# A transformer block with expert retrieval: six more expert blocks made ahead, four block buffers, and another order and pacing of VectorE's work

## The chip, the cores and the metric

The kernel runs on one core of a Trainium2 chip. The metric is the device time of one execution in microseconds (us), lower is better. The time before is the median of three runs.

## The reference, cut to what matters

One encoder block on 1024 tokens of width 1024: attention and a convolution first, then a retrieval layer over 16384 experts (128 blocks of 128). The second half is what the change touches:

```
def _peer(xn, peer_wq, peer_keys, peer_u, peer_v):
    ...
        q = (xc @ peer_wq).reshape(TOKEN_CHUNK, PEER_HEADS, PEER_DQ)
        s1 = jnp.einsum('chd,nd->chn', q[..., :half], peer_keys[0])
        s2 = jnp.einsum('chd,nd->chn', q[..., half:], peer_keys[1])
        v1, i1 = lax.top_k(s1, PEER_TOPK)
        v2, i2 = lax.top_k(s2, PEER_TOPK)
        ...
        top_s, pos = lax.top_k(cand_s, PEER_TOPK)
        e = jnp.take_along_axis(cand_i, pos, axis=-1)
        g = jax.nn.softmax(top_s, axis=-1).astype(xc.dtype)
        u = peer_u[e]
        h = jax.nn.gelu(jnp.einsum('cd,chkd->chk', xc, u))
        return jnp.einsum('chk,chkd->cd', g * h, peer_v[e])
```

Each token picks 16 experts for each of 8 heads, 128 in all.

## The kernel before, in words

The 1024 tokens are 8 tiles of 128. Two methods share the retrieval layer.

**Gathered tiles.** Tiles 0, 1 and 2 (`NG = 3`) take the direct way: for each of the 128 picks of a token, GpSimd issues an indirect DMA (L1154) that fetches one row of 1024 values for each of 128 tokens, and VectorE multiplies and sums it (L1187, for `peer_u`) or adds it with its weight (L1199, for `peer_v`). That is 3 x 256 = 768 gathers. `class Gather` keeps their order, 7 row slots and the pointer `nc`.

**Dense tiles.** Tiles 3 to 7 (640 tokens, `TD`) take the dense way: all 128 blocks of 128 experts are multiplied with all tokens. For a block, 48 matmuls (8 slices of the width, 3 passes of a split in two halves, 2 token halves) give the block's activations, ScalarE applies Gelu, VectorE multiplies them with the gate matrix, and matmuls with the block's `peer_v` rows add the result into the outputs. The gate matrix is built from the picks by matmuls of one-hot matrices, 160 groups of four tokens, and stored in DRAM (`GD`).

The program's order is written out by hand, and the instructions of an engine run in the order in which they are issued. Four stages follow each other.

1. Attention, convolution and projections, up to the scores of the retrieval (`wgen`), which are stored in DRAM (`SD`).
2. The **second stage**, the loop that calls `gpe`, `ustep`, `gpost` and `kadv`. An iteration issues one one-hot group on TensorE (`gpe`: three matmuls for the differences, L1082 to L1085, and eight for the product, L1100), a quarter of an activation block that is made ahead (`ustep`: 12 matmuls, L1236), ScalarE's work for the one-hot groups (`gprep`, L1091 and L1093, and `gevac`, L1110, which copies the product into one of five buffers `gblk`; every eighth iteration stores four of them, L1113), and then some of VectorE's work (`kadv`). The loop ends when all 160 groups are done. Blocks made ahead are stored in DRAM (`HDm`).
3. A short **junction**: the last two ahead blocks, the first loads and splits of the last stage.
4. The **last stage**, a loop over blocks i = 0 to 126. An iteration has three slots. A slot holds `rotate` (six matmuls of 512 columns over two blocks into the one PSUM tile `prot`, which VectorE then adds into the output X, L1561), `accum` (three matmuls, in the third slot six, into `acc`), and `ugroup` (12 matmuls, L1496, a quarter of an activation block that was not made ahead). Between them stand VectorE's gate products (L1479, L1487) and the gathers, which are spread evenly over the iterations (`gat.adv`).

**What sets the order around the change.** `K0` blocks are made ahead (their indices are `US`, evenly spread), all but `KT = 2` of them in the second stage: `KM = K0 - KT`, so 31 blocks and 124 calls of `ustep`. The other 95 blocks (`ulist`) are made in the last stage, 380 quarters for 381 slots. `kadv` keeps a credit for VectorE: an iteration adds its modelled length (3.05), and each step of VectorE's work that `kstep` issues takes its price off: 2.0 for a head of the first top-k (`topk1`), 1.3 or 1.8 for the pieces of the second (`topk2`, L986 at its start, L1037 near its end), `GCOST = 3.0` for a gather. `kstep` takes the second top-k before the first one and gathers last, but after a piece of the second top-k lets another kind go first. `korder` is the order of the tiles in both top-ks: dense tiles' picks feed the one-hot groups, gathered tiles' picks feed the gathers, and no gather can be issued until the picks of tile 0 are there. Inside `topk2` a dense tile's values go through ScalarE (the exponential at L1012, then 24 copies into `L`, spread over nine iterations by `HOLD`), in ScalarE's order ahead of its one-hot work.

The multiply of a `peer_u` gather writes its full product, which nobody reads, into the third part of the tile `QB` (`jk`); only the sum is kept. The activations of the last stage live in three buffers (`hfree`): two tiles and the first part of `QB`. A buffer is taken by `hload` (a block made ahead is loaded, L1453) or by `ugroup` (Gelu writes it), and given back by `amake2`. `uahead` splits the next block's weights into two halves (`usplit`: a copy on ScalarE, L116, and a subtraction on GpSimd, L119) once an iteration.

Of the kernel before, what the change touches and what calls it, by code (L numbers as in the profile page):

```python
# [10 lines left out]
BF = mybir.dt.bfloat16  # L11
# [3 lines left out]
ALU = mybir.AluOpType  # L15
# [16 lines left out]
NK = 128  # L32
# [9 lines left out]
NPERS = 4  # L42
K0 = 33
WIN = 2
NVI = 3
NO2 = 2
GPE = 1.4
GCOST = 3.0
KT = 2
# [22 lines left out]
def peer_block(tc, I, out):  # L72
# [54 lines left out]
    with ExitStack() as fr:  # L127
# [55 lines left out]
        with ExitStack() as st:  # L183
# [186 lines left out]
            for j, nm in enumerate(["q_norm_g", "k_norm_g"]):  # L370
                a = I[nm]
# [120 lines left out]
        with ExitStack() as st:  # L492
# [272 lines left out]
            for u in range(NU + 4):  # L765
                g = (u + 4) // 4
# [350 lines left out]
    class Gather:  # L1117
# [51 lines left out]
        def adv(self, n=1):  # L1169
            for _ in range(n):  # L1170
# [7 lines left out]
                if ph == 0:  # L1178
                    h = self.h(t) if ps is None else ps
                    if k == 0:  # L1180
                        self.hh[t] = gp.tile([P, P], F32, name=f"hh{t}")
                        if ps is not None:
                            self.stage(t)
                            A.copy(ps, self.staged[t])
                            self.slots.append(self.staged.pop(t))
                    jk = QB[:, 2, :].bitcast(BF)
                    V.scalar_tensor_tensor(jk, r, 1.0, h, op0=ALU.mult, op1=ALU.mult,  # L1187
                                           accum_out=self.hh[t][:, k:k + 1])
# [57 lines left out]

    korder = [3, 4, 5, 0, 6, 7, 1, 2]
    ks = dict(n1=0, n2=0, gen=None, ld=0, credit=0.0, last="")
# [36 lines left out]
    def k_gat():  # L1285
        if not ks.get("gat") or not gat.ready():
            return None
        gat.adv(1)
        return GCOST

# [52 lines left out]
    ust = dict(i=0, seg=0, hps=None, prev=None)  # L1343

    def ustep():
        i = ust["i"]
        if i >= KM:
            return 0.0
        if i == 0 and ust["seg"] == 0:
# [54 lines left out]
    while True:  # L1404
# [6 lines left out]
        kadv(dt, dt)  # L1411
    ho = gelu_(ust["prev"], up, 1)
    SY.dma_start(HDm[KM - 1], ho[:])
    while ks["n2"] < len(korder):
# [4 lines left out]
    with ExitStack() as vs:  # L1419
# [47 lines left out]
        hfree = [vp.tile([P, TD], F32, name=f"ho{j}")[:] for j in range(2)]  # L1467
        hfree.append(QB[:, 0:2, :].rearrange("p a b -> p (a b)")[:, :TD])

# [45 lines left out]
        ulist = [i for i in range(NK) if i not in UI]  # L1515
        ug = dict(g=0, split=0, load=0, ps=None)

# [9 lines left out]
        def ugroup():  # L1527
# [3 lines left out]
            i, (hf, d) = ulist[m], divmod(q, 2)  # L1531
            if ug["split"] <= m:
                uahead()
            if d == 0:
                ug["ps"] = ubank()
            uhalf(i, hf, ug["ps"], d * DC // 2, (d + 1) * DC // 2)
            if d == 1:
                if hf == 0:
                    HO[i] = hfree.pop(0)
                ugelu(HO[i], hf, ug["ps"])  # L1540
            ug["g"] += 1

        def uready(i):
# [56 lines left out]
        for i in range(NK - 1):  # L1600
# [9 lines left out]
            vsplit(nx)  # L1610
            uahead()
            rs_ = [w for w in range(len(rot)) if i % WIN == w % WIN]
            rotate(rs_[0], i, False)
            accum(i, (0,))
            ugroup()
            gat.adv(gs[0])
            rotate(rs_[1], i, False)
            accum(i, (1,))
            ugroup()
            uready(nx)  # L1620
# [4 lines left out]
            accum(i, (2, 3))  # L1625
            ugroup()
            gat.adv(gs[2])
# [73 lines left out]
```

## Time and profile before

| | |
|---|---|
| median of 3 runs | 2993.06 us (2991.23 to 2999.02) |
| the profiled execution | 2996.14 us, span 2994.4 us, mean granted TensorE clock 0.979 |
| busy over the span | TensorE 2799.0 us (93%), VectorE 2463.6 (82%), GpSimd 1953.6 (65%), ScalarE 1149.2 (38%) |
| DMA | 710.33 MB, mean 237 GB/s |
| chain of work that ended last | TensorE 55%, VectorE 20%, DMA 8%, issue 7% |

A busy time is the time in which an engine had at least one instruction in work; matmuls overlap, and their ends are modelled. In a row of the trace, PE is TensorE's matmuls, PEld its weight loads, DVE VectorE, ACT ScalarE, POOL GpSimd, SPq the DMA queue that SyncE issues. "a <- b" names what was waited for; L numbers are lines of the kernel.

### The profile page before, as it was taken

What the parts mean: (1) busy time and instruction counts of PE and PEld (TensorE: products, weight loads), DVE (VectorE), ACT (ScalarE), POOL (GpSimd) and SP (SyncE); (2) the same over time, 40 slices, a digit from 0 to 9 for tenths busy, and PEclk for the clock granted to TensorE, in tenths of its full rate; (3) what the DMA queues carried; (4) which work ended last, traced back from release to release, by engine and by line L of the source; (5) the groups of instructions that cost most, each with busy time, mean ns of one, the idle gap of its engine ahead of it and who ended that gap; (6) DMA issues with size and microseconds to landing.
All of it is one profiled execution on the core that took longest, in us unless ns stands there. A gap on an engine that the chain in (4) does not pass through costs nothing.

```text
span 2994.4 us, 44528 instructions
## 1 busy us (share of the span) xinstructions
PE 2799.0 (93%) x16042; PEld 2475.3 (83%) x16048; DVE 2463.6 (82%) x4465; ACT 1149.2 (38%) x2376; POOL 1953.6 (65%) x1558
## 2 busy tenths in 40 slices
PE   7878899899989899978999999999999999999997
PEld 6767778698978788867888888888888888888886
DVE  5889988468666967864899988988899999999998
ACT  3216566342577577663222222222222222222222
POOL 2578842104445766764777777777777777777775
PEclk9989999999999999999999999999999999999999
DMA  4111000044334667676899898999999998989996
GB/s 131 46 68 36 8 1 15 33 159 129 106 142 149 219 228 266 211 276 251 330 336 345 332 337 330 349 334 353 335 348 335 349 347 333 341 333 337 341 342 228
DMA packets 296719, 710.33 MB, mean 237 GB/s; under 512 B 25264, under 2 KB 135216, under 8 KB 296368
## 3 DMA queue, kind: packets, MB, share of 16 engines
q0 software_dynamic: 110592, 402.70, 35.2%
q1 hardware_dynamic: 156800, 252.85, 25.1%
q10 hardware_dynamic: 29104, 51.91, 4.6%
q8 instruction: 126, 2.06, 0.3%
q14 instruction: 97, 0.79, 0.1%
HBM read 640.46 MB, written 66.91 MB: 236 GB/s over the span
## 4 chain that ended last, share of the span: by engine, by line
PE 55%; DVE 20%; DMA 8%; issue 7%; POOL 4%; ACT 4%; ACTq 1%; SPq 0%; another core or an unknown queue 0%; POOLq 0%; DVEq 0%
PE hps L1496 15%; PE hps L1236 5%; PE prot L122 5%; PE prot L123 4%; PE prot L124 4%; DVE y L146 3%; PE pg L1100 3%; PE acc L122 3%; PE acc L124 3%; PE acc L123 3%; DMA rows<-peer_v,ei 2%; DMA rows<-peer_u,ei 2%; DVE ga L1199 2%; DVE ho L1479 2%; DVE PT L119 2%
## 5 line engine op out<-in xcount | busy, mean ns | idle before, releaser
L1496 PE MATMUL hps<-HN,uh 128*128 128x320 f32 x3072 | 683.9, 310 | 8.1 <-ACT ho L1243 5.3
L1496 PEld LDWEIGHTS hps<-HN,uh 128*128 128x128 f32 x3072 | 530.4, 189 | 42.4 <-issue 5.5
L1496 PE MATMUL hps<-HN,ul 128*128 128x320 f32 x1536 | 475.6, 310 | 0.0
L1199 DVE SCALAR_TENSOR_TENSOR ga<-rows,aa,ga 128x1024 f32<-128x1024 f32 x330 | 424.0, 1285 | 27.5 <-DMA rows<-peer_v,ei 18.1
L1154 POOL DMA_INDIRECT rows<-peer_u,ei x339 | 360.1, 1062 | 108.0 <-issue 68.7
L119 POOL TENSOR_TENSOR vl<-vr,vh 128x1024 fp32r<-128x1024 f32 x128 | 308.8, 2413 | 156.9 <-ACT vh L116 108.5
L1154 POOL DMA_INDIRECT rows<-peer_v,ei x330 | 326.9, 991 | 112.6 <-issue 72.5
L1187 DVE SCALAR_TENSOR_TENSOR QB<-rows,ga 128x1024 bf16<-128x1024 f32 x271 | 329.7, 1216 | 31.3 <-DMA rows<-peer_u,ei 25.1
L122 PE MATMUL prot<-vh,ah 128*128 128x512 f32 x762 | 309.0, 406 | 27.9 <-DVE X L1561 18.6
L119 POOL TENSOR_TENSOR ul<-ur,uh 128x1024 fp32r<-128x1024 f32 x127 | 324.5, 2555 | 2.6
L1561 DVE TENSOR_TENSOR X<-X,prot 128x512 f32<-128x512 f32 x384 | 262.1, 682 | 65.5 <-PE prot L124 55.2
L123 PE MATMUL prot<-vl,ah 128*128 128x512 f32 x762 | 301.1, 395 | 0.4 <-POOL vl L119 0.4
L124 PE MATMUL prot<-vh,al 128*128 128x512 f32 x762 | 297.5, 390 | 0.0
L1496 PEld LDWEIGHTS hps<-HN,ul 128*128 128x128 f32 x1536 | 289.5, 188 | 0.0
L1506 ACT ACTIVATE ho<-hps 128x320 f32<-128x320 f32 x128 | 55.8, 436 | 493.3 <-PE hps L1496 456.2
L1110 ACT COPY gblk<-pg 128x128 f32<-128x128 f32 x640 | 175.6, 440 | 99.2 <-PE pg L1100 74.2
L116 ACT CAST vh<-vr 128x1024 fp32r<-128x1024 f32 x128 | 133.7, 1045 | 203.3 <-DMA vr<-peer_v 196.0
L1236 PE MATMUL hps<-HN,uh 128*128 128x320 f32 x992 | 210.0, 334 | 0.0
L122 PE MATMUL acc<-vh,ah 128*128 128x512 f32 x512 | 199.6, 390 | 0.0
L124 PE MATMUL acc<-vh,al 128*128 128x512 f32 x512 | 199.6, 390 | 0.0
L123 PE MATMUL acc<-vl,ah 128*128 128x512 f32 x512 | 199.5, 390 | 0.0
L122 PEld LDWEIGHTS prot<-vh,ah 128*128 128x128 f32 x762 | 143.2, 188 | 65.7 <-DVE X L1561 32.6
(273 smaller groups left out, 6550.0 us busy)
## 6 DMA issues: line engine op xcount, KB each, us to landing
ur<-peer_uT SPq DMA_DIRECT2D x128, 512.0 KB
vr<-peer_v SPq DMA_DIRECT2D x128, 512.0 KB
GD<-gblk ACTq DMA_DIRECT2D x80, 512.0 KB
gl<-GD SPq DMA_DIRECT2D x64, 640.0 KB
wqr<-peer_wq SPq DMA_DIRECT2D x32, 512.0 KB
HDm<-ho SPq DMA_DIRECT2D x31, 320.0 KB
s<-SD SPq DMA_DIRECT2D x64, 128.0 KB
ho<-HDm SPq DMA_DIRECT2D x22, 320.0 KB
```

Of the source, the lines that this page charges most:

```text
L116: A.copy(hi, src)
L119: lo_eng.tensor_tensor(lo, src, f(hi), op=ALU.subtract)
L122: PE.matmul(ps, ah, bh, start=start, stop=False)
L123: PE.matmul(ps, ah, bl, start=False, stop=False)
L124: PE.matmul(ps, al, bh, start=False, stop=stop)
L1110: A.copy(gblk[b][k][:, :, q * 4:q * 4 + 4].rearrange("p i t -> p t i"), pg[:, :, k * w:k * w + w])
L1154: G.indirect_dma_start(out=r, out_offset=None, in_=I["peer_v" if ph else "peer_u"], in_offset=bass.IndirectOffsetOnAxis(ap=ge[t][:, k:k + ...
L1187: V.scalar_tensor_tensor(jk, r, 1.0, h, op0=ALU.mult, op1=ALU.mult, accum_out=self.hh[t][:, k:k + 1])
L1199: V.scalar_tensor_tensor(to, r, self.aa[t][:, k:k + 1], to, op0=ALU.mult, op1=ALU.add)
L1236: PE.matmul(hps[:, j, :b - a], (uh, uh, ul)[st3][:, dc, :], HN[(0, 1, 0)[st3]][:, dc, a:b], start=dc == 0 and st3 == 0, stop=dc == DC - 1 ...
L1496: PE.matmul(ps[:, :b - a], (uh, uh, ul)[st3][:, dc, :], HN[(0, 1, 0)[st3]][:, dc, a:b], start=dc == 0 and st3 == 0, stop=dc == DC - 1 and ...
L1561: V.tensor_tensor(X[:, NG + t, n:n + 512], X[:, NG + t, n:n + 512], pr, op=ALU.add)
```

## The change

It makes 39 instead of 33 blocks ahead (37 of them, 148 calls of `ustep`, in the second stage), so 89 are left for the last stage (356 quarters for 381 slots). `uslot` issues a quarter only when the count of quarters lags an even spread over all slots, and not when it would need the last free buffer. The product of a `peer_u` gather is written over the gathered row itself; the whole of `QB` then gives two activation buffers, four in all. `uahead` moves from the start of an iteration to behind the first quarter of a block. Tile 0 comes third in `korder` instead of fourth, tile 5 fourth. A gather costs 2.0 of credit. `ulast` stores the last ahead block of the second stage.

```diff
-K0 = 33
+K0 = 39
...
-GCOST = 3.0
+GCOST = 2.0
+GCOST2 = 2.0
...
-                    jk = QB[:, 2, :].bitcast(BF)
-                    V.scalar_tensor_tensor(jk, r, 1.0, h, op0=ALU.mult, op1=ALU.mult,
+                    V.scalar_tensor_tensor(r, r, 1.0, h, op0=ALU.mult, op1=ALU.mult,
                                            accum_out=self.hh[t][:, k:k + 1])
...
-    korder = [3, 4, 5, 0, 6, 7, 1, 2]
+    korder = [3, 4, 0, 5, 6, 7, 1, 2]
...
-        return GCOST
+        return GCOST if ks["n2"] < len(korder) else GCOST2
...
+    def ulast():
+        if ust["prev"] is not None:
+            ho = gelu_(ust["prev"], up, 1)
+            SY.dma_start(HDm[KM - 1], ho[:])
+            ust["prev"] = None
+
     def ustep():
         i = ust["i"]
         if i >= KM:
+            ulast()
             return 0.0
...
-        hfree.append(QB[:, 0:2, :].rearrange("p a b -> p (a b)")[:, :TD])
+        hfree += [QB[:].rearrange("p a b -> p (a b)")[:, j * TD:(j + 1) * TD] for j in range(2)]
...
-            if ug["split"] <= m:
-                uahead()
             if d == 0:
                 ug["ps"] = ubank()
...
             ug["g"] += 1
+            if q == 0:
+                uahead()
+
+        def uslot():
+            ug["slot"] += 1
+            if ug["g"] < -(-4 * len(ulist) * ug["slot"] // (3 * (NK - 1))) and (ug["g"] % 4 != 1 or len(hfree) > 1):
+                ugroup()
...
             vsplit(nx)
-            uahead()
             rs_ = [w for w in range(len(rot)) if i % WIN == w % WIN]
             rotate(rs_[0], i, False)
             accum(i, (0,))
-            ugroup()
+            uslot()
...
             accum(i, (1,))
-            ugroup()
+            uslot()
...
             accum(i, (2, 3))
-            ugroup()
+            uslot()
```

## Rows read from the trace of the kernel before

**Rows 1.** Busy time by stretch: span bounds, length, each engine's busy time, clock, DMA share, GB/s
```profile
853.50:1295.10 441.60, 417.67 (x2844) 376.73 (x2843) 331.13 (x1189) 310.37 (x868) 284.84 (x230) 0.99 0.60 210
1295.10:1363.20 68.10, 46.42 (x259) 33.18 (x257) 38.51 (x50) 48.10 (x145) 32.64 (x22) 0.89 0.68 250
1363.20:1399.70 36.50, 33.16 (x176) 30.79 (x177) 14.75 (x24) 10.63 (x15) 17.99 (x12) 0.88 0.75 259
1399.70:2962.70 1563.00, 1543.49 (x8271) 1364.48 (x8270) 1416.69 (x1756) 383.39 (x541) 1215.15 (x907) 1.00 0.91 338
```

**Rows 2.** Chain that ended last, second stage: start, length, engine, tile, line
```profile
1041.10 0.91 PE pg L1100 x8
...
1151.47 0.91 PE pg L1100 x8
...
1200.31 1.75 PE hps L1236 x12
1203.60 1.76 PE hps L1236 x12
...
1356.74 1.17 PE pg L1100 x8
```

**Rows 3.** Groups by line and shape, 853 to 1363 us: busy, mean ns, idle before
```profile
L1110 ACT COPY gblk<-pg 128x128 f32<-128x128 f32 x592 | 162.5, 441 | 94.9 <-PE pg L1100 74.2 <-DMA GD<-gblk 18.1 <-remote 2.2
L1187 DVE SCALAR_TENSOR_TENSOR QB<-rows,QB 128x1024 bf16<-128x1024 f32 x68 | 100.0, 1471 | 26.7 <-DMA rows<-peer_u,ei 26.0 <-issue 0.2
L1154 POOL DMA_INDIRECT rows<-peer_u,ei x73 | 90.6, 1241 | 20.7 <-issue 12.7 <-DVE QB L1187 1.4 <-DVE z L1032 1.3
L119 POOL TENSOR_TENSOR ul<-ur,uh 128x1024 fp32r<-128x1024 f32 x30 | 84.1, 2805 | 2.4
```

**Rows 4.** Waits in the second stage and, last, of SyncE's queue in the last stage
```profile
ACT d L1012 <- DVE d L1011: 4.9, 1, 4.9
...
POOL uh L118 <- PE hps L1236: 103.4, 19, 17.4
...
SPq L1453 <- DVE ho L1479: 459.2, 21, 24.5
```

**Rows 5.** VectorE in order of time: start and end of tile 6's and tile 7's second top-k
```profile
977.72 0.45 DVE L986 CAST xf<-ix 128x256 f32<-128x256 uint32 x1
...
1039.94 0.29 DVE L1037 TENSOR_TENSOR g<-d,rz 128x128 f32<-128x128 f32 x1
...
1074.47 1.23 DVE L986 CAST xf<-ix 128x256 f32<-128x256 uint32 x1
...
1144.35 1.91 DVE L1037 TENSOR_TENSOR g<-d,rz 128x128 f32<-128x128 f32 x1
```

**Rows 6.** Chain that ended last, an iteration of the last stage
```profile
1611.23 1.75 PE hps L1496 x12
1612.99 0.23 PE prot L122
...
1615.05 1.75 PE hps L1496 x12
...
1619.55 1.75 PE hps L1496 x12
```

**Rows 7.** Groups by line, 1399.7 to 2962.7 us
```profile
L1199 DVE SCALAR_TENSOR_TENSOR ga<-rows,aa,ga 128x1024 f32<-128x1024 f32 x327 | 420.1, 1285 | 27.4 <-DMA rows<-peer_v,ei 18.1 <-issue 2.7 <-DVE X L1561 0.9
L1187 DVE SCALAR_TENSOR_TENSOR QB<-rows,ga 128x1024 bf16<-128x1024 f32 x265 | 322.4, 1216 | 29.8 <-DMA rows<-peer_u,ei 23.6 <-issue 2.1 <-DVE X L1561 0.4
L1561 DVE TENSOR_TENSOR X<-X,prot 128x512 f32<-128x512 f32 x376 | 256.6, 682 | 60.3 <-PE prot L124 50.1 <-issue 8.6
L122 PEld LDWEIGHTS prot<-vh,ah 128*128 128x128 f32 x752 | 141.1, 188 | 53.3 <-DVE X L1561 22.0 <-issue 7.7 <-DVE ga L1199 4.0
```

**Rows 8.** Line L1435, a multiply that writes whole f32 rows: ns min/median/max
```profile
L1435 DVE SCALAR_TENSOR_TENSOR rows<-X,rs,rows x6: 1277/1278/1283, 2972.0 to 2987.2; 128x1024 f32<-128x1024 f32 x6
```

**Rows 9.** TensorE in order of time at the start of the junction
```profile
1364.97 0.73 PE L1496 MATMUL hps<-HN,uh 128*128 128x320 f32 x2
...
1365.77 0.73 PE L1496 MATMUL hps<-HN,uh 128*128 128x320 f32 x2
```

More of the change, by code (lines that the diff above doesn't have):

```diff
@@ L1411, in peer_block @@
         kadv(dt, dt)
-    ho = gelu_(ust["prev"], up, 1)
-    SY.dma_start(HDm[KM - 1], ho[:])
+    ulast()
     while ks["n2"] < len(korder):
@@ L1515, in peer_block @@
         ulist = [i for i in range(NK) if i not in UI]
-        ug = dict(g=0, split=0, load=0, ps=None)
+        ug = dict(g=0, split=0, load=0, ps=None, slot=1)
         def uahead():
```

## The prediction

> **What bounds the kernel now.** I read the busy time by stretch first, because the shares of the whole span mix stages with different limits. In the last stage TensorE is busy for 1543.5 of 1563.0 us, VectorE for 1416.7 (90.6%), and the DMA engines for 91% [rows 1]: TensorE sets the time, with two others close behind. In the second stage TensorE is busy for 417.7 of 441.6 us, until its last ahead block ends at 1295.1. Then follow 68.1 us in which only one-hot groups are left and TensorE is busy for 46.4 us at a granted clock of 0.89 [rows 1]. Those 68 us are the room that the change wants to fill. 124 of the loop's iterations hold a quarter block, and the loop has 148: 13 of the 160 groups are done in stage one, 147 are left, one an iteration, and one iteration drains. 37 blocks are 148 quarters, so the new ones fill exactly the 24 bare iterations, and the loop gets no longer in count.
>
> **Second stage, six blocks added.** The chain of waits shows two neighbouring quarters 3.29 us apart, and the same point four batches of eight iterations later 110.4 us apart, so 3.45 us an iteration with the batch's stores [rows 2]. The last one-hot group starts 61.6 us after 1295.1 [rows 2]. With quarters in them, the same 23 intervals take 23 x 3.45 = 79.4 us: **+18 us**. The ends are 23 x 3.29 = 75.7 (+14) and 23 x 3.56 = 81.9 (+20), the mean of the first 124 (441.6/124). The waits of ScalarE for stores of the gate matrix, 18.1 us [rows 3], lie mostly in the bare iterations and shrink with the slower pace; that is in the 3.45. Six more block stores and loads stand on SyncE's queue here, as before one a block.
>
> **Second stage, gathers and order.** Following the credits step by step through the pacing code gives 68 gathers before the loop ends, which is what the trace has [rows 3], and 108 after: 40 more, all of tile 0's first half. They cost VectorE 40 x 1.47 = 59 us and GpSimd 40 x 1.24 = 50 us, and six more subtractions cost GpSimd 17 us [rows 3]. VectorE is busy for 331.1 + 38.5 = 369.6 of 509.7 us now; it would be 429 of some 528 (81%). GpSimd's queue, which carries casts, subtractions, top-k sums and gathers in one order, waits 103.4 us for TensorE to free a weight buffer [rows 4]; the 67 us fit into that. So on average neither bounds. What counts is where ScalarE stands waiting for VectorE inside the second top-k, with the one-hot work queued behind it and TensorE behind that. Before, this cost 4.9 us once [rows 4]. By the credits, a dense tile's second top-k gets 16 iterations from its start to its hand-over in place of 18, because gathers go by faster and tile 0 no longer comes between the dense tiles: 55 us for what took VectorE 62.2 and 69.9 us [rows 5]. Some of those were waits for GpSimd that TensorE held back. I take **+4 us**, between 0 and 44 (three tiles, 7 and 15 us late each). One head of the first top-k slips from stage one into stage two; it is in that share.
>
> A gather's multiply takes 1471 ns in the second stage, where both operands lie in SBUF, and 1216 ns in the last stage, where one lies in PSUM [rows 3, 7]: 0.255 us more for each of the 40, 10 us of VectorE's time that the move costs, already in the 59. The Trainium skill (SBUF — State Buffer, section "Who interferes with whom") has a rule for it, and it speaks against this move: a VectorE instruction with two SBUF inputs contends with a GpSimd instruction that reads SBUF, and the second to issue waits. By that rule more GpSimd work in the stage makes every such multiply, the old ones too, longer still.
>
> **Last stage, 24 quarters less.** Here a quarter takes 1.76 us from its start to the next matmul, and an iteration without a stall 3.82 + 4.50 + 3.82 = 12.14 us [rows 6]. 24 x 1.76: **-42 us**. VectorE loses 40 gathers at 1.30 (52 us) and the DMA 40 rows' worth and net one block's worth of bytes (22 MB, 65 us at the 338 GB/s of [rows 1]). All three near-limits go down by at least what TensorE does, so none takes over by its sum.
>
> **The gaps that the missing quarters leave.** `prot` is one PSUM tile: the next rotation cannot start until VectorE has added the last one. A quarter and three `accum` matmuls cover that now for 2.28 us (0.52 without the quarter; 1.20 in the third slot). The addition takes 0.68 us [rows 7] and ends 0.73 us after the rotation if VectorE is free: 0.2 us of stall. If a gather of 1.29 us has just begun, 1.5 us. Stepping the even spread through gives 8, 9 and 7 skips in the three slots: 17 x 0.85 + 7 x 0.4 = 17 us. I take **+14**, since VectorE's load falls to (1417 - 52)/(1563 - 31) = 89%; ends 5 and 42, the second being all that was saved. The stalls of this kind that exist, 22.0 us before the rotation's weights [rows 7], shrink with the load: **-3** (0 to -10).
>
> **Junction and clock.** The junction's first matmuls run with the triplets 0.80 us apart where 0.44 (a quarter of the 1.76) is the pace later, at a granted clock of 0.88, after TensorE had idled; some six triplets [rows 9]. With the stage before filled, TensorE comes in busy: **-2 us**.
>
> **Edits that I cost at nothing.** The product written as a whole f32 row: a multiply with such an output takes 1278 ns against 1216 [rows 8, 7]; 276 of the last stage's would cost 17 us at most, and none at least; VectorE's idle 146 us there cover it, and without that cover it would add to the gaps. `uahead` one to three slots later: a split then leads its block by three slots (11.5 us), more than its copy and subtraction of under 4 us; if a load came late, the block's first matmul would wait. The fourth buffer: `hload` waits 459 us in SyncE's queue for a buffer [rows 4], with weight loads behind it, but none of TensorE's long waits is for a weight; it makes the even spread possible, no more. `ulast`: one Gelu in the same place.
>
> **Sum.** 18 + 4 - 42 + 14 - 3 - 2 = -11 us, against the profiled execution's 2996.1 us. That one lies 3.1 us above the median, so on the median's scale 2993 - 11 = 2982 us.
>
> **The rivals.**
> (1) *Slower: ScalarE waits for VectorE at each dense tile's hand-over.* If the three second top-ks need the measured 62 to 70 us in 55, the loop loses 7 to 15 us at each, 33 us in the middle in place of my 4: -11 - 4 + 33 = +18, so 3011 us. It decides from a total lateness of some 24 us on. For it speak the two spacings [rows 5] and the longer multiplies; against it VectorE's 72% load and the 103 us for which GpSimd waits.
> (2) *No change that can be told.* The second stage grows by 20 + 8 and the gaps give back 16, with no relief for the old stalls: 28 - 42 + 16 - 2 = 0, so 2993 us. For it speaks that each term is only somewhat worse than mine.
> (3) *A larger gain.* VectorE's lower load closes most gaps: 14 + 0 - 42 + 5 - 6 - 2 = -31, so 2962 us. For it speaks that VectorE is relieved by more than TensorE; against it that a skipped slot always leaves at least 0.2 us.
> By the skill's rule alone, the second stage's old 68 multiplies would rise by a like 0.25 us, 17 us of VectorE's time, an estimate; that is a push towards rival 1, and its chance includes it.
>
> **How the numbers follow.** My forecast has 0.40 and covers 2972 to 2984. Rival 2 has 0.28 (2984 to 3002), rival 3 0.17 (below 2972), rival 1 0.15 (above 3002). 0.3% is 9 us, about what a measurement of this kernel can tell from no change. So faster has 0.40 + 0.17 = 0.57, the same 0.28, slower 0.15. The range leaves out a tenth at each side: 2964, near rival 3's middle, to 3004, into rival 1.
>
> **What would show it.** 108 gathers with their target row as output before the junction, and 37 ahead blocks; the quarters of the last 24 iterations 3.4 to 3.5 us apart and the junction's start near 1379 to 1386 us; a granted clock near 1.00 at that start. The last stage shorter by 25 to 36 us, with VectorE's share at 89% or less, and waits of the rotation for VectorE's addition up by some 10 us. I am wrong on the second stage if ScalarE waits for VectorE (L1012, L1063) by 20 us or more, and wrong on the last stage if it shrinks by under 20 us or by the full 42.

## The result, and the profile after

The kernel became slower: 3077.32 us in the median of five runs (3062.88 to 3084.38) against 2993.06, a ratio of 1.0275 (1.0248 to 1.0302). I had forecast 2982, and the result lies outside my range. The profiled execution took 3062.88 us, 66.7 more than that of before (2996.14); it is the fastest of the five, 14.4 us under the median.

Busy time by stretch of the changed kernel, with the columns of [rows 1] (PE, PEld, VectorE, ScalarE and GpSimd busy, granted clock, DMA share, GB/s): second stage, junction, last stage, end.

```profile
858.60:1397.00 538.40, 499.06 (x3390) 449.50 (x3388) 459.34 (x1399) 361.60 (x1012) 408.33 (x317) 0.98 0.69 246
1397.00:1433.00 36.00, 27.74 (x145) 25.79 (x146) 9.56 (x17) 8.67 (x13) 15.98 (x11) 0.86 0.85 301
1433.00:3027.20 1594.20, 1520.57 (x8006) 1338.75 (x8005) 1355.61 (x1685) 372.86 (x525) 1164.54 (x866) 0.99 0.88 319
3027.20:3061.10 33.90, 17.26 (x63) 13.06 (x61) 23.55 (x27) 11.05 (x19) 7.85 (x16) 0.75 0.31 125
```

Against [rows 1], the start of the second stage moved by 5.1 us (858.6 for 853.5), the second stage grew by 28.7 (509.7 to 538.4), the junction went from 36.5 to 36.0, and the end grew by 2.2. **The last stage, with 24 quarter blocks less to do, grew by 31.2 us** (1563.0 to 1594.2), where I had forecast about 31 less. In it TensorE stands idle for 73.6 us (1594.2 - 1520.6) in place of 19.5, VectorE's share fell from 90.6% to 85%, and the DMA's from 0.91 to 0.88. No engine took over as the bound: everything waits more.

Where the waits are. Waits in the last stage of the changed kernel, 1450 to 3020 us (us in total, times, longest), and under them those of SyncE's own DMA queue:

```profile
ACT vh L117 <- DMA vr<-peer_v: 242.6, 38, 13.4
POOL vl L120 <- ACT vh L117: 182.8, 41, 11.5
PEld prot L123 <- DVE X L1572: 71.0, 59, 5.2
PE prot L123 <- DVE X L1572: 50.8, 38, 4.8
PE hps L1502 <- ACT ho L1512: 12.8, 6, 6.1
...
SPq L1218 <- POOL ul L120: 902.8, 76, 18.4
SPq L1459 <- DVE ho L1485: 311.4, 34, 20.0
SPq L1463 <- POOL vl L120: 78.9, 19, 10.5
SPq L1463 <- DMA vr<-peer_v: 39.2, 9, 6.9
```

L1459 is the load of the gate matrix `gl` (L1453 before), L1463 the load of a block's `peer_v` rows `vr` (L1457), L117 ScalarE's copy that splits them (L116). ScalarE had waited for `vr` before, too. Its queue in order of time, before, at each fourth block:

```profile
1574.57 1.05 ACT L116 CAST vh<-vr 128x1024 fp32r<-128x1024 f32 x1 [6.60 <-DMA vr<-peer_v]
1624.26 1.06 ACT L116 CAST vh<-vr 128x1024 fp32r<-128x1024 f32 x1 [6.36 <-DMA vr<-peer_v]
1674.49 1.05 ACT L116 CAST vh<-vr 128x1024 fp32r<-128x1024 f32 x1 [7.18 <-DMA vr<-peer_v]
1724.78 1.05 ACT L116 CAST vh<-vr 128x1024 fp32r<-128x1024 f32 x1 [6.84 <-DMA vr<-peer_v]
```

and after:

```profile
1568.75 1.05 ACT L117 CAST vh<-vr 128x1024 fp32r<-128x1024 f32 x1 [6.14 <-DMA vr<-peer_v]
1624.82 1.04 ACT L117 CAST vh<-vr 128x1024 fp32r<-128x1024 f32 x1 [13.41 <-DMA vr<-peer_v]
1674.36 1.05 ACT L117 CAST vh<-vr 128x1024 fp32r<-128x1024 f32 x1 [6.28 <-DMA vr<-peer_v]
1726.64 1.05 ACT L117 CAST vh<-vr 128x1024 fp32r<-128x1024 f32 x1 [5.42 <-DMA vr<-peer_v]
...
2337.41 1.05 ACT L117 CAST vh<-vr 128x1024 fp32r<-128x1024 f32 x1 [10.79 <-DMA vr<-peer_v]
```

Before, one such wait stands every 50 us, that is every fourth iteration, and nearly all of them are 6 to 7 us long. After, they swing between 1 and 13 us. What happens in the longest of them, SyncE's queue first, then ScalarE, VectorE and TensorE, in order of time (start, length; in brackets the idle time before it and what ended it):

```profile
1603.97 0.33 SPq L1218 DMA_DIRECT2D ur<-peer_uT  x1
1604.34 6.29 SPq L1459 DMA_DIRECT2D gl<-GD  x2
1610.68 5.27 SPq L1463 DMA_DIRECT2D vr<-peer_v  x2
...
1610.69 0.73 ACT L1487 CAST ah<-ho 128x640 fp32r<-128x640 f32 x1 [2.43 <-DVE ho L1485]
1624.82 1.04 ACT L117 CAST vh<-vr 128x1024 fp32r<-128x1024 f32 x1 [13.41 <-DMA vr<-peer_v]
1625.77 0.43 ACT L1512 ACTIVATE ho<-hps 128x320 f32<-128x320 f32 x1
...
1609.75 0.90 DVE L1485 TENSOR_TENSOR ho<-ho,gl 128x320 f32<-128x320 f32 x2
...
1626.26 0.90 PE L1502 MATMUL hps<-HN,uh 128*128 128x320 f32 x2 [6.11 <-ACT ho L1512]
```

Read from the top. The gate load comes in two halves and has three buffers, so its second half has to wait until VectorE's gate product of the block before (L1485, 1609.75) gives a buffer back. SyncE's queue is in order: the `vr` load, which needs nothing from the gate, is issued only at 1610.68, and its data are there at 1624.8, 14 us later (over the whole run a `vr` load lands after 8.4 us in the median). ScalarE is in order as well: it stands at the copy of `vr` for 13.41 us, and behind that copy stands the Gelu (L1512) that empties TensorE's one bank `hps`. So TensorE waits 6.11 us for a bank that ScalarE could have emptied long before.

In the kernel before, the `vr` load stands behind the gate load as well, but there the first gate half has gone out long ahead of it:

```profile
1744.11 23.35 SPq L1453 DMA_DIRECT2D gl<-GD  x2
1767.56 0.60 SPq L1457 DMA_DIRECT2D vr<-peer_v  x1
```

In the changed kernel a weight load (L1218) had held the queue until 1604, because GpSimd's subtraction had not yet freed its buffer. SyncE's waits from 1600 to 1620 us:

```profile
SPq L1218 <- POOL ul L120: 13.5, 1, 13.5
```

So both gate halves went out just ahead of `vr`. From 1450 to 2900 us the two halves are issued 21.7 us apart in the median before, and 10.0 us after. ScalarE's copy then starts 8.0 us after the issue of its `vr` load in the median before, and 10.8 us after (15.8 at most). That it is the bytes of the gate halves that hold up `vr` is inferred from these times. All this is a theory up to here; the runs test it.

### The profile page after: what moved, and what is told of

It is laid out like the page before. It is cut to its first block, busy times and chain, and to the rows that moved or that the text cites. A ratio compares the mean times of both kernels' runs of the same rounds, so it can differ in the third digit from the quotient of the medians.

```text
span 3061.1 us, 44188 instructions
## 1 busy us (share of the span) xinstructions
PE 2811.5 (92%) x16042; PEld 2489.9 (81%) x16048; DVE 2478.6 (81%) x4465; ACT 1140.6 (37%) x2362; POOL 1983.6 (65%) x1564
## 5 line engine op out<-in xcount | busy, mean ns | idle before, releaser
L1502 PEld LDWEIGHTS hps<-HN,uh 128*128 128x128 f32 x2880 | 500.9, 190 | 61.3 <-ACT ho L1512 15.3
L1155 POOL DMA_INDIRECT rows<-peer_u,ei x345 | 384.2, 1114 | 105.8 <-issue 57.8
L1502 PE MATMUL hps<-HN,ul 128*128 128x320 f32 x1440 | 448.1, 311 | 0.0
L1187 DVE SCALAR_TENSOR_TENSOR rows<-rows,ga 128x1024 f32<-128x1024 f32 x237 | 282.1, 1212 | 22.4 <-DMA rows<-peer_u,ei 19.6
L1502 PEld LDWEIGHTS hps<-HN,ul 128*128 128x128 f32 x1440 | 273.3, 190 | 0.0
L117 ACT CAST vh<-vr 128x1024 fp32r<-128x1024 f32 x128 | 133.9, 1046 | 243.5 <-DMA vr<-peer_v 243.0
L1236 PEld LDWEIGHTS hps<-HN,uh 128*128 128x128 f32 x1184 | 195.0, 191 | 21.7 <-issue 0.8
L1187 DVE SCALAR_TENSOR_TENSOR rows<-rows,QB 128x1024 f32<-128x1024 f32 x108 | 168.6, 1586 | 40.5 <-DMA rows<-peer_u,ei 40.4
```

Source lines behind the costliest of these rows:

```text
L117: A.copy(hi, src)
L1155: G.indirect_dma_start(out=r, out_offset=None, in_=I["peer_v" if ph else "peer_u"], in_offset=bass.IndirectOffsetOnAxis(ap=ge[t][:, k:k + ...
L1187: V.scalar_tensor_tensor(r, r, 1.0, h, op0=ALU.mult, op1=ALU.mult, accum_out=self.hh[t][:, k:k + 1])
L1236: PE.matmul(hps[:, j, :b - a], (uh, uh, ul)[st3][:, dc, :], HN[(0, 1, 0)[st3]][:, dc, a:b], start=dc == 0 and st3 == 0, stop=dc == DC - 1 ...
L1502: PE.matmul(ps[:, :b - a], (uh, uh, ul)[st3][:, dc, :], HN[(0, 1, 0)[st3]][:, dc, a:b], start=dc == 0 and st3 == 0, stop=dc == DC - 1 and ...
```

## The experiments

Ratios are against the kernel before, run alongside on the same chip. The fifth and sixth columns are from the profiled execution: the first matmul of the junction, and the time from there to the end of the span. The last is ScalarE's wait for `vr` from 1450 to 2900 us (total, times, longest).

| kernel | median us | ratio | interval | first junction matmul | from there | wait for `vr` |
|---|---|---|---|---|---|---|
| before | 2993.06 | 1 | | 1363.2 | 1631.2 | 180.7, 28, 7.2 |
| changed | 3077.32 | 1.0275 | 1.0248 to 1.0302 | 1397.0 | 1664.1 | 232.9, 36, 13.4 |
| e1 split back | 3076.16 | 1.0298 | 1.0261 to 1.0336 | 1397.6 | 1674.3 | 203.8, 30, 13.2 |
| e2 before + moved split | 3034.12 | 1.0151 | 1.0116 to 1.0185 | 1361.8 | 1665.8 | 199.8, 26, 12.0 |
| e3 old pacing | 3078.97 | 1.0282 | 1.0253 to 1.0311 | 1381.2 | 1708.1 | 239.0, 36, 14.5 |
| e4 before + new pacing | 3001.70 | 1.0039 | 1.0026 to 1.0052 | 1380.3 | 1617.2 | 188.0, 29, 8.0 |
| e5 changed, `vr` first | 2984.93 | 0.9955 | 0.9940 to 0.9971 | 1401.7 | 1590.0 | 16.8, 13, 3.0 |
| e6 before, `vr` first | 2962.53 | 0.9883 | 0.9863 to 0.9903 | 1362.6 | 1594.7 | none |
| e7 e1 with `vr` first | 2969.83 | 0.9906 | 0.9886 to 0.9926 | 1398.7 | 1569.3 | 4.4, 4, 1.4 |
| e8 e1 with 33 blocks | 3011.92 | 1.0050 | 1.0034 to 1.0065 | 1390.9 | 1616.5 | 187.0, 29, 7.7 |
| e9 e7 with old pacing | 2953.82 | 0.9877 | 0.9855 to 0.9898 | 1377.4 | 1567.3 | 3.8, 4, 2.2 |
| e10 e7 with old order, price 2.0 | 2977.28 | 0.9947 | 0.9928 to 0.9966 | 1386.4 | 1575.1 | 4.0, 5, 1.2 |
| e11 e9, gaps in third slots | 2953.33 | 0.9866 | 0.9843 to 0.9889 | 1382.5 | 1573.6 | 7.2, 5, 2.0 |
| e12 e6 with f32 row | 2956.74 | 0.9878 | 0.9857 to 0.9898 | 1367.2 | 1593.7 | none |
| e13 e6 again | 2956.43 | 0.9875 | 0.9860 to 0.9890 | 1361.2 | 1593.6 | none |
| e14 e9 again | 2950.51 | 0.9860 | 0.9841 to 0.9879 | 1375.3 | 1573.4 | 4.5, 5, 1.5 |
| e16 e2 with `vr` first | 2964.79 | 0.9895 | 0.9880 to 0.9910 | 1365.4 | 1602.7 | 4.9, 3, 2.5 |

**One part undone or done alone.** e1 takes `uahead` back to the start of an iteration in the changed kernel; e2 makes that move alone in the kernel before:

```diff
-            if ug["split"] <= m:
-                uahead()
...
+            if q == 0:
+                uahead()
...
-            uahead()
             rs_ = [w for w in range(len(rot)) if i % WIN == w % WIN]
```

> The changed kernel with one edit undone: the split and load of the next weight block stand at the start of an iteration again, behind the iteration's peer_v load, as before. Theory (late loads): the moved load waits in SyncE's queue for a GpSimd subtraction in the middle of an iteration, the peer_v load behind it is issued late, ScalarE stands still for it (longest wait 13.4 us) and VectorE and TensorE with it. Then the last stage (1433.0 to 3027.2 us, 1594.2 us in the changed kernel, 1563.0 before) falls to 1535 to 1550 us, ScalarE's longest wait for a peer_v load to 8 us or less, and the time to 3010 to 3030 us. Rival (gaps): the skipped quarters leave VectorE's addition uncovered, wherever the split stands: last stage within 15 us of 1594, time 3060 to 3085 us. Rival (second stage): the second stage's 28 us and a busier DMA make the loss; no change in the last stage either.

> The kernel before with only that edit made: the split and load of the next weight block stand behind the first quarter of a block; 33 blocks ahead, three buffers, no skipped quarter. Theory (late loads): 20 to 60 us slower than before, 3013 to 3053 us, ScalarE's longest wait for a peer_v load above 10 us. Rival (gaps): no quarter is skipped, so within 9 us of before. Rival (second stage): within 9 us of before.

The two answers look like a contradiction: alone the move costs 1.5%, and undone in the changed kernel it gives nothing back. My first theory, that late weights from the move explain the loss, fell with e1. Something else in the changed kernel does the same damage: in both, as in the changed kernel, ScalarE's longest wait for `vr` is 12 to 13 us.

e3 puts the old `korder` and the old price of 3.0 for a gather into the changed kernel, e4 the new ones into the kernel before:

```diff
-GCOST = 2.0
-GCOST2 = 2.0
+GCOST = 3.0
+GCOST2 = 3.0
...
-    korder = [3, 4, 0, 5, 6, 7, 1, 2]
+    korder = [3, 4, 5, 0, 6, 7, 1, 2]
```

> The changed kernel with the old order of the tiles and the old price 3.0 of a gather (71 gathers ahead of the last stage in place of 108). Theory (late loads): the second stage loses its early stalls and gets 10 to 15 us shorter, the last stage, with 37 more gathers on VectorE, stays slow or gets longer by up to 15 us: 3062 to 3080 us. Rival (second stage): 3000 to 3030 us, since the second stage and what it hands on is the loss.

> The kernel before with only the order of the tiles and the price 2.0 of a gather (94 or so gathers ahead in place of 68). Theory (late loads): stage one and the second stage 5 to 15 us longer, the last stage equal or up to 10 us shorter: 2990 to 3008 us. Rival (second stage): 3020 us and more.

Both put the same price on the pacing in the second stage: 1397.6 - 1381.2 = 16.4 us between e1 and e3, 1380.3 - 1363.2 = 17.1 us between e4 and before (17.8 and 14.5 us, counted from the first matmul of each second stage). In e4, with 33 blocks, the time from the junction on gave 14.0 of it back (1631.2 to 1617.2), and the ratio is 1.0039. The pacing is not what made the last stage longer.

**The queue's order.** One edit in `loads`, in the changed kernel (e5), in the kernel before (e6) and in e1 (e7):

```diff
+                vload(i)
                 if i % GCH == 0:
                     gload(i)
-                vload(i)
```

> The changed kernel with one exchange in SyncE's order: every fourth iteration loads gate blocks (gl) and a peer_v block (vr); the peer_v load now goes first. Theory (drift): with 3 quarters an iteration, four iterations are three blocks, and a weight load of SyncE's queue always met the gate loads in the same place; with 2.8 quarters, or with the moved split, it meets them everywhere, both gate halves and then the peer_v block come late together, and ScalarE stands up to 13.4 us for every fourth peer_v block (6 to 8 us before, always the same). If that is the loss, ScalarE's waits for peer_v above 8 us vanish, the last stage falls from 1594 us by 40 us or more and the time to 3005 to 3040 us. Rival (gaps): within 15 us of the changed kernel, 3060 to 3085 us. Rival (buffers): a buffer of the four, or the product written over the row, is at fault: no change either.

> The kernel before with that exchange alone. Theory (drift): ScalarE's 29 waits of 6 to 7 us for a peer_v block vanish, but TensorE was busy for 99% of the last stage, so the time stays or gains up to 12 us: 2980 to 2996 us. Rivals (gaps, buffers): no change, 2984 to 3001 us.

> The changed kernel with the split back at the start of an iteration and the peer_v load first. Theory (drift): as in the run with the exchange alone or somewhat better, since the weights too come in time: 2995 to 3030 us. Rival (gaps): 3055 to 3080 us. Rival (buffers): 3055 to 3080 us.

The same instructions, the same bytes and the same buffers, in another order in SyncE's queue, took 3.1% from the changed kernel (ratio 1.0275 to 0.9955), 3.8% from e1 (1.0298 to 0.9906) and 1.2% from the kernel before. All three gained more than I had expected. e5's waits in the last stage, from 1450 to 2900 us, beside those shown above:

```profile
PEld prot L123 <- DVE X L1572: 30.4, 34, 4.5
PE prot L123 <- DVE X L1572: 17.1, 14, 4.3
ACT vh L117 <- DMA vr<-peer_v: 16.8, 13, 3.0
```

ScalarE's wait for `vr` all but vanishes, and with it more than half of TensorE's waits for VectorE's addition (PE 45.4 us over the same stretch of the changed kernel, 17.1 here). VectorE had been late in part because ScalarE was: its subtraction at L1493 needs ScalarE's copy `ah`, which also stood behind `vr` (48.5 us of such waits in the changed kernel, 17.4 in e5). With the queue mended, 24 fewer quarters do what was forecast: from the junction on, e7 takes 1569.3 us and e6 1594.7, 25.4 less.

**A second way of the same fault.** The exchange also shortened VectorE's own work: from the junction on it was busy for 1452.9 us before and for 1345.8 us in e13 (e6 once more), with the same 1803 instructions. What shrank is the gate product. The groups by line over the whole run: the gate product of before and of e7, then the subtraction behind it in the changed kernel and in e7.

```profile
L1479 DVE TENSOR_TENSOR ho<-ho,gl 128x320 f32<-128x320 f32 x172 | 176.3, 1063 | 14.1 <-DMA gl<-GD 10.4 <-DMA ho<-HDm 1.9 <-ACT ho L1506 1.8
...
L1485 DVE TENSOR_TENSOR ho<-ho,gl 128x320 f32<-128x320 f32 x130 | 75.6, 621 | 20.4 <-DMA gl<-GD 18.5 <-DMA ho<-HDm 1.9
...
L1493 DVE TENSOR_TENSOR al<-QB,ah 128x640 fp32r<-128x640 f32 x63 | 90.9, 1443 | 34.9 <-ACT ah L1487 34.6
...
L1493 DVE TENSOR_TENSOR al<-QB,ah 128x640 fp32r<-128x640 f32 x63 | 51.6, 820 | 8.5 <-ACT ah L1487 5.6 <-issue 2.0 <-ACT ho L1512 0.8
```

Both read two inputs from SBUF. From 1450 to 2900 us, a gate product takes 489 ns in the median before and 485 in e13. But 111 of 232 took over 620 ns before, up to 3143, and each of these began while GpSimd was in a subtraction of L119; above the median they cost 132 us. In e13 it is 68 of 238, up to 1400 ns, and 24 us. The addition at L1561, which reads one input from PSUM, took 689 ns at most in both, beside the same subtractions. So the place of the `vr` load also decides where GpSimd's subtractions fall on VectorE's work. No run separates this way from ScalarE's standing still: both go when the two loads are exchanged.

**Why the fault grew.** The kernel before made three quarters in each iteration. A gate load comes every four iterations, and four iterations were exactly three blocks, so a weight load always stood at the same place beside a gate load. With 356 quarters in 381 slots, 2.8 an iteration, the two drift past each other. The queue shows it: between two gate loads (1435 to 2910 us) the `vr` and weight loads come in one and the same order all 29 times before, and in five different orders in the changed kernel and in e1. e8 tests what that does: e1 with all its edits, but 33 blocks.

```diff
-K0 = 39
+K0 = 33
```

> The changed kernel with the split back at the start of an iteration and 33 blocks ahead as before: four buffers, the product written over the row, the new order and pacing stay, but four iterations are three blocks again and no quarter is skipped. Theory (drift): as the kernel before with the new order and price alone, 2992 to 3012 us, and ScalarE's waits for peer_v are 6 to 8 us each. Rival (gaps): the same, 2992 to 3012 us. Rival (buffers): 3040 us or more.

It ran at 1.0050, 2.5% under e1, and the last stage is that of e4 again (1616.5 and 1617.2 from the junction on). ScalarE's queue in e8:

```profile
1701.88 1.05 ACT L117 CAST vh<-vr 128x1024 fp32r<-128x1024 f32 x1 [6.31 <-DMA vr<-peer_v]
1750.42 1.05 ACT L117 CAST vh<-vr 128x1024 fp32r<-128x1024 f32 x1 [6.09 <-DMA vr<-peer_v]
1800.50 1.05 ACT L117 CAST vh<-vr 128x1024 fp32r<-128x1024 f32 x1 [6.80 <-DMA vr<-peer_v]
1848.93 1.05 ACT L117 CAST vh<-vr 128x1024 fp32r<-128x1024 f32 x1 [6.12 <-DMA vr<-peer_v]
```

The waits are even again, and the queue's order is the same all 29 times, with the f32 row, the four buffers and `uslot` all in place. So none of these lengthened the last stage; the number of blocks did. With 33 blocks no quarter is left out, so e8 alone could not tell the rhythm from the gaps. e7 does: it has 39 blocks and the gaps, and its last stage is short.

**What is left of the change.** e9 is e7 with the old pacing, e10 e7 with the old `korder` alone, and e11 is e9 with left-out quarters only in the third slot:

```diff
             ug["slot"] += 1
-            if ug["g"] < -(-4 * len(ulist) * ug["slot"] // (3 * (NK - 1))) and (ug["g"] % 4 != 1 or len(hfree) > 1):
+            due = ug["slot"] % 3 != 1 or ug["g"] < -(-4 * len(ulist) * ug["slot"] // (3 * (NK - 1)))
+            if due and (ug["g"] % 4 != 1 or len(hfree) > 1):
                 ugroup()
```

> The changed kernel with the weight split back at the start of an iteration, the peer_v load ahead of the gate loads (2969.8 us so), and now the old order of the top-k steps and 3.0 for a gather: what is left of the change is the six blocks, the four buffers and the f32 row. Theory A (the new pacing is what the second stage lost beyond the blocks; it cost 17 us alone, 2993 to the junction at 1380 against 1363): the first junction matmul starts near 1382 and the time is 2950 to 2957, below the 2962.5 of the kernel before with the load moved. Theory B (the second stage's loss comes from the blocks and the wider row, and what the pacing costs there it gives back in the last stage by gathers done earlier): the junction starts near 1397 or the last stage grows by as much, and the time stays at 2966 to 2973.

> The same as the run before it, but with 2.0 for a gather kept: only the order of the top-k steps goes back. It splits the pacing's cost between its two parts. If the price of a gather carries it (gathers put too close on VectorE, which is then late for the one-hots), the time is within 5 us of 2969.8 and the junction starts near 1395. If the place of the first gathered tile's top-k carries it (VectorE's scores and one-hots wait at the start of the stage), it is within 5 us of the run with both back, near 2955, junction near 1382.

> As the run with the old order and price, but a quarter block is left out only in the third slot of an iteration, never in the first two. 25 left-out quarters cost 16.8 us in gaps between matmuls in the changed kernel, where ones in the third slot cost the least. Theory A (such a gap is set by what VectorE has still to do at that slot): the gaps shrink by half and the time falls by 5 to 10 us against the run without this edit. Rival (a gap is the wait for the buffer of the next rotation, wherever the quarter is missing, or the drift of the weight loads decides): the same time within 3 us.

e9 lies in the middle of theory A: 2953.8, though its junction started even earlier than forecast. It is 16 us under e7 by the medians, but the two were not run side by side: by the ratios it is some 9 us, and the intervals meet. e10 gave neither of its two answers: it is slower than e7 by 0.4% and than e9 by 0.7%, and its runs spread from 2963 to 2980 us. By the times, the price of 2.0 costs some 20 us with the old order, and the new order takes part of that back. By the junction's start it is otherwise: 9.0 us from e9 to e10 for the price, 12.3 us from e10 to e7 for the order. So how the cost divides between the two stays open; the new order at the old price was not run. e11 equals e9 (0.9866 and 0.9877), and TensorE's idle time from the junction on did not shrink (39.5 us, 30.8 in e9): where the missing quarters lie does not matter here, and the rival was right.

e12 puts the f32 row alone into e6:

```diff
-                    jk = QB[:, 2, :].bitcast(BF)
-                    V.scalar_tensor_tensor(jk, r, 1.0, h, op0=ALU.mult, op1=ALU.mult,
+                    V.scalar_tensor_tensor(r, r, 1.0, h, op0=ALU.mult, op1=ALU.mult,
```

> The kernel before with the peer_v load ahead of the gate loads (2962.5 us so) and one more edit: the gather's product is written over its f32 row rather than as bf16 into a spare piece; buffers, blocks and pacing stay as before. Theory A (the wider write is slower only while other engines write as well, 1586 ns for 1471 in the second stage over some 68 gathers of four parts, and VectorE is not what the stage waits for): 2962 to 2967, junction within 3 us of 1362.6. Rival (the 10 us that the changed code cost in the second stage with no further block come from this write): 2970 to 2975, junction near 1371.

It costs nothing that the times show: 0.9878, where e6 has 0.9883. The junction of its profiled execution started 4.6 us later than e6's, outside the 3 us that I had allowed; that execution was 5.9 us over the run's median. In the second stage its multiplies were not even longer. The groups by line, first of e12, then of e6:

```profile
L1186 DVE SCALAR_TENSOR_TENSOR rows<-rows,QB 128x1024 f32<-128x1024 f32 x68 | 92.3, 1373 | 34.8 <-DMA rows<-peer_u,ei 34.7
```

```profile
L1187 DVE SCALAR_TENSOR_TENSOR QB<-rows,QB 128x1024 bf16<-128x1024 f32 x68 | 97.5, 1434 | 23.4 <-DMA rows<-peer_u,ei 22.0 <-issue 0.8
```

**Side by side.** e13 and e14 are e6 and e9 once more, run alongside each other; e16 is e2 with `vr` first.

> The kernel before with the peer_v load ahead of the gate loads, once more, on the same chip and in the same rounds as the next one. Earlier it took 0.9883 of the time before (0.9863 to 0.9903), so 2956 to 2964 here; it is the measure for the next run.

> The changed kernel with that load mended, the split at the start of an iteration and the old pacing (0.9877 of the time before, 0.9855 to 0.9898, in another call), side by side with the run before it. Theory A (with the queue in order the six blocks cost 18 in the second stage and give back 26 to 31 in the last, as was forecast): 6 to 14 us less than the run before it. Theory B (what is left of a missing quarter is eaten by gaps and by a busier VectorE): within 4 us of it.

> The kernel before with the moved split, which alone cost 41 us, and the peer_v load ahead of the gate loads. Theory A (the move costs through the peer_v load's place behind the gate loads in SyncE's queue): at most 15 us above the mended kernel without the move, so 2957 to 2977, and ScalarE's waits for that load under 30 us. Rival (the move costs by itself, a weight that comes too late for its block or a split in the way of VectorE and ScalarE): again some 40 us above it, 2995 to 3005.

e16 settles the contradiction of e1 and e2: with `vr` first, the move that had cost 42 us costs 8 (2964.8 against 2956.4). Its way of harm is the same queue. A split that comes later also frees its weight buffer later, and the weight load that waits for that, in front of the gate and `vr` loads, holds SyncE's queue for longer (in the kernel before 663 us of such waits from 1450 to 2900, in e2 797). There is no drift in e2: the order is the same at all 28 gate loads, but the two gate halves are 9.6 us apart in the median in place of 21.7.

e13 and e14 differ by 5.9 us in the median (0.9875 and 0.9860), and their intervals overlap: with the queue mended, the six blocks, the four buffers and the f32 row cannot be told from no change, and are worth 0.15% by the ratios. Four of e14's five runs do lie below all of e13's. Where the difference comes from shows in the busy time up to the junction and from there on. First e13, then e14:

```profile
850.00:1361.20 511.20, 465.97 (x3128) 410.63 (x3129) 381.73 (x1303) 365.86 (x1034) 322.32 (x265) 0.98 0.60 215
1361.20:2954.80 1593.60, 1570.28 (x8496) 1407.76 (x8496) 1345.78 (x1803) 401.60 (x574) 1249.01 (x934) 0.99 0.91 340
```

```profile
850.00:1375.30 525.30, 499.87 (x3400) 450.08 (x3399) 386.13 (x1274) 366.79 (x1025) 346.68 (x266) 0.99 0.61 218
1375.30:2948.70 1573.40, 1538.15 (x8208) 1363.70 (x8208) 1347.09 (x1797) 394.19 (x556) 1217.18 (x925) 0.99 0.92 344
```

288 matmuls (24 quarters of 12) left the second stretch. The first grew by 14.1 us, since 19.8 of TensorE's 33.9 new busy us filled idle time. The second shrank by 20.2: 32.1 of busy time less, 11.9 of idle time more. 20 - 14 is the gain of 6.

Both e6 and e9 beat the two kernels of this study, by 1.2% each over the one before.

## Why the prediction was wrong

**The step that failed** is the sum of "Last stage, 24 quarters less": "All three near-limits go down by at least what TensorE does, so none takes over by its sum". It went by the busy time of the engines, and the one path that did take over, SyncE's queue with ScalarE behind it, I had put at nothing in "Edits that I cost at nothing", in two sentences. On the fourth buffer I wrote that "`hload` waits 459 us in SyncE's queue", "but none of TensorE's long waits is for a weight". The row is L1453, which is `gload`, not `hload` (that is L1473, with 6.9 us of waits from 1450 to 2900): I had put it down to the wrong load. I named the weight loads behind it and not the `vr` load, which stands right behind the gate load in the code. And I asked whether TensorE waits for a load, where ScalarE did: 180.7 us at the `vr` copy, which I had not looked for in this stage. On `uahead` I named a cover for the matmuls (three slots) and not what the later weight load holds up in its queue. Neither sentence asked what keeps the loads in their places: three quarters an iteration, four iterations a gate load. The change took that rhythm away. The price: 1.0275 to 0.9955 with one line moved, some 96 us, where the same line gives the kernel before 34.6 (2997.1 to 2962.5 side by side).

The last stage came out 62 us above the forecast. Of these, 43 are idle time of TensorE (73.6 us, where 19.5 + 14 - 3 = 30.5 was forecast) and 19 are busy time (1520.6 us, where 1543.5 - 42 = 1501.5 was forecast). In this stage the granted clock fell to half, 1.2 GHz, twelve times, for 44 us in all, which costs 22 us of full speed; in the last stage of before it never fell.

**What bounds the kernel.** "TensorE sets the time" was too trusting. The kernel before from the junction on, to be read against e13's second row above:

```profile
1363.20:2994.40 1631.20, 1591.10 (x8496) 1405.94 (x8496) 1452.86 (x1803) 405.07 (x574) 1240.99 (x934) 0.99 0.90 332
```

TensorE's 1591.1 busy us fell to 1570.3 in e13 with the same 8496 matmuls, and its idle time from 40.1 (1631.2 - 1591.1) to 23.3. More than half of the 37.6 us that came free had been shown as busy. The clock does not explain that, since it did not fall in the last stage of before; how TensorE came to be shown as busy there stays open.

**Second stage, six blocks: +18.** Right in its size. The junction starts 18.0 us later in e3 than in before, and 14.1 later in e14 than in e13. Counted from the first matmul of each second stage it is 11.4 and 18.2 us. There are 37 ahead blocks, as forecast.

**Second stage, gathers and order: +4, between 0 and 44.** 16 to 17 (e1 against e3, e4 against before): within the bounds, the taken value too low. One wait of VectorE goes with the new order: in the six kernels that have it (changed, e1, e4, e5, e7, e8) VectorE stands for 21.3 to 21.6 us for scores from DRAM, just ahead of the second stage, and in no other kernel for more than 8.5. What that wait costs was not separated. The 108 gathers came as counted:

```profile
L1187 DVE SCALAR_TENSOR_TENSOR rows<-rows,QB 128x1024 f32<-128x1024 f32 x107 | 167.4, 1589 | 40.5 <-DMA rows<-peer_u,ei 40.4
L1155 POOL DMA_INDIRECT rows<-peer_u,ei x110 | 149.0, 1355 | 33.1 <-issue 17.8 <-DVE rows L1187 6.4 <-DVE gs L1056 3.3
```

(107 multiplies lie wholly within these bounds.) A multiply takes 1589 ns in the mean for the 1471 of [rows 3], a gather 1355 for 1241. But the mean hides two kinds. The same multiplies, ns min/median/max, before and after:

```profile
L1187 DVE SCALAR_TENSOR_TENSOR QB<-rows,QB x68: 1204/1225/3285, 974.2 to 1335.5; 128x1024 bf16<-128x1024 f32 x68
...
L1187 DVE SCALAR_TENSOR_TENSOR rows<-rows,QB x108: 1205/1223/3407, 915.6 to 1397.5; 128x1024 f32<-128x1024 f32 x108
```

Half of them take what a multiply with an input in PSUM takes (1216 ns [rows 7]), so the 0.255 us of the prediction is no cost that each of them has. 18 of 68 before and 38 of 107 after took over 1.3 us, and 17 and 33 of these began while GpSimd was in a tensor operation or a cast; of the other 50 and 69 it was 3 and 1. A gather that GpSimd was issuing mattered little: 19 of 20 and 26 of 30 multiplies that began beside one kept the short time. In the mean a multiply became 0.12 us longer, 13 us over 108 of them. The Trainium skill (SBUF — State Buffer, section "Who interferes with whom") says that a VectorE instruction with two SBUF inputs contends with a GpSimd instruction that reads SBUF. The trace agrees; the 0.12 us are about half of the 0.25 us that I had worked out by that rule. The mean does not go by the number of gathers: e4, with 103, has a mean of 1466 ns, e14, with 71, has 1533, and five kernels with the second stage of before have 1418 to 1477. The write of the f32 row is not the cause, by e12 (1373).

**Rival 1** came true in its sign only. ScalarE's wait for VectorE at L1013 is 12.5 us after, for 4.9 (16.7 with L1064), under the 20 that I had named as the mark. The loss came from a place that no rival of mine named.

**Last stage, 24 quarters, gaps, relief: -31.** The terms come near where the queue is in order: -25.4 (e7 against e6), -20.2 (e14 against e13), both counted from the junction on; the second is at the mark of 20 that I had named. The extra gaps were +11.9 between e13 and e14, where I had +14. They are not what I took them for, though: had VectorE's load in each slot set them, e11 should have closed half.

**Junction and clock: -2.** The junction took 36.0 us for 36.5, and its granted clock was 0.86 for 0.88. No gain there. TensorE came in at 1.00, as forecast, and ran for 7.2 us; then it stood for 6.4 us until ScalarE's Gelu (L1512) had run, which itself had waited 7.8 us for a store of the gate matrix.

**Left open.** The first 5.1 us, up to the start of the second stage: kernels that change nothing in that part began at 853.5 to 858.2, so it is not a cost that I can put down to the change. Why the moved split still costs 8 us with `vr` first (and 15 in the changed kernel, e5 against e7) was not settled. A small cost of the f32 row in the second stage is not excluded: from its first matmul to the junction, e12 took 511.2 us and e6 504.8, and e8 took 531.8 and e4 524.2, where five kernels with one and the same second stage spread from 503.6 to 509.7. A fourth gate buffer, the other cure of the wait, was not tried.

## What to carry to other kernels

A DMA queue in program order is a path like an engine: when a load may have to wait for a buffer, ask which loads stand behind it, and put first those whose buffers are free. Before changing how much is done in an iteration, look for pairs of periods that fit each other (here three quarters an iteration and a gate load every four); a wait of constant length at a constant interval is the sign of such a pair, and a small change of rate turns it into a drift. An engine that looks 99% busy can still give back time, so read the waits of all engines in the stage that matters, the lightly loaded ones first.

## What the runs showed that I had not expected

- TensorE is shown as busy for 98.8% of the last stage before (1543.5 of 1563.0 us), and still the order of two loads took 36.5 us out from the junction on (e6: 1594.7 for 1631.2).
- ScalarE, busy for 24% of the last stage (383.4 of 1563.0 us), held up an engine with 99%: it was never short of time, only of order.
- After the wait at 1620 to 1626 us, TensorE's granted clock was 0.74 over the next 10 us, for 1.00 ten us before and ten us later; busy time by stretch of the changed kernel:

```profile
1606.00:1616.00 10.00, 10.00 (x54) 8.82 (x53) 8.93 (x11) 1.17 (x2) 7.34 (x7) 1.00 1.00 333
1616.00:1626.00 10.00, 4.15 (x23) 3.39 (x21) 6.03 (x8) 1.18 (x2) 0.11 (x2) 0.92 0.78 298
1626.00:1636.00 10.00, 9.74 (x41) 8.88 (x42) 5.20 (x5) 2.66 (x5) 8.93 (x6) 0.74 0.45 131
1636.00:1646.00 10.00, 10.00 (x56) 8.97 (x55) 8.53 (x11) 3.43 (x5) 8.62 (x7) 1.00 1.00 371
```

In these ten us 41 matmuls ran at a busy share of 97%, where 54 to 56 run at the full clock. So a stall of six us costs more than its own length, and the rest of it is counted as busy.
